# Lower projections of fifteen feed-forward pairs by Strassen's algorithm, with weight block sums made by accumulating transfers

## The chip, the cores and the metric

The kernel runs on one core of a Trainium2 chip. Time is the device time of one execution in microseconds (us); the time of a kernel is the median of its runs. The engines are TensorE (PE, matmuls; PEld is its weight load), VectorE (DVE), ScalarE (ACT), GpSimd (POOL) and SyncE (SP, which here only issues transfers).

## The reference

A trunk of two layers on 512 tokens and 1024 channels, all in float32. Layer 0 is a convolution module and a SwiGLU feed-forward part; then one set of keys and values is projected for the second layer; layer 1 is sliding-window attention and a second feed-forward part; a last normalisation ends it. Cut to what the change touches:

```python
def swiglu_ffn(x, w_up, w_down):
    gate, up = jnp.split(x @ w_up, 2, axis=-1)
    return (jax.nn.silu(gate) * up) @ w_down

for l in range(DEPTH):
    if l < N_A_LAYERS:
        h = h + conformer_conv(rmsnorm(h, norm_mix[l]), ...)
    else:
        if l == N_A_LAYERS:
            kv = rmsnorm(h, norm_kv) @ w_kv
        q = rmsnorm(h, norm_mix[l]) @ w_q[j]
        h = h + banded_sink_attention(q, k, v, sinks[j], rel_bias) @ w_o[j]
    h = h + swiglu_ffn(rmsnorm(h, norm_ffn[l]), w_up[l], w_down[l])
return rmsnorm(h, norm_final)
```

x is 512 x 1024, w_up 1024 x 5632 (gate and up), w_down 2816 x 1024.

## The kernel before

Everything is held transposed: channels on the 128 partitions, tokens along the free dimension. The running state h is eight tiles of 128 x 512. The hidden size of 2816 is eleven pairs of two 128-row tiles.

Each float32 factor is split into a high part in the faster float32r form and a low rest, and a product is three matmuls (`mm3`, L344 to L347): high by high, high by low, low by high. The activations are split once. The weights come as chunks of 128 x 1024 (512 KB): SP loads one into a `raw` tile, ACT casts it into `whi`, and DVE subtracts to get `wlo` (`split_chunk`, L261 to L271). There are four buffers each of `raw`, `whi` and `wlo`, so the cast of a chunk waits until PE has ended with the chunk four before it. `PLAN` is the list of all chunks in the order of use; `get` (L319) hands out the next one and first calls `advance`, which loads up to 6 chunks ahead and splits up to 3 ahead.

A feed-forward layer runs in parts of two to four pairs (`HALVES0`, `HALVES1`): all upper products of the part, then its lower projections, which add into h. The first two pairs of a layer are plain (`ffn_up`). All later pairs use Strassen's algorithm in Winograd's form for the upper products (`ffn_prod`, L573): seven products j = 0 to 6 on half-size blocks, which accumulate in three PSUM banks a, b and c, with moving factors of 256 tokens. The seven right factors (sums of blocks of the normalised state, `right_factors`) are formed once a layer. The left ones are weight blocks and their sums: `load_block` loads two blocks into `raw` and two into a `blocks` tile, and `block` (L219) forms S1, S3 and two more sums on DVE, two at j = 1 (L227, L228) and two at j = 2 (L231, L232).

The lower projections are plain (`down_group`, L468): for each half g of the output rows four banks of 128 x 512, for each pair two inner tiles, four row tiles, three matmuls of 512 tokens; then DVE adds each bank into h (L488). At the end of layer 0, `on_h` makes the normalised and split input of keys and values from each finished row tile (L458, L459) and POOL adds up its squares (L423).

The order of instructions on each engine is made by a scheduler ahead of time, and each engine runs its own list in order; PE's list mixes the next product in where the scheduler saw a use for it. So the order can be read, and does not change while the kernel runs.

Of the kernel before, what the change touches and what calls it, by code (L numbers as in the profile page):

```python
# [54 lines left out]
def chunk_plan():  # L55
# [42 lines left out]
    for kp in range(*LAST):  # L98
        for g in range(2):
# [4 lines left out]
PLAN = chunk_plan()  # L104
CHUNKS = [c for c in dict.fromkeys(PLAN) if c[0] != "prod"]
CHUNKS += [("up", layer, pair, half, which) for layer in range(2) for pair in range(PLAIN[layer], FT // 2)
           for which in range(2) for half in range(2)]
CHUNK_AT = {c: i for i, c in enumerate(CHUNKS)}


def lay_weights(w):
    out = np.empty((len(CHUNKS), P, 1024), np.float32)
    q = w["w_q"][0][:, HEAD_COLS]
    o = w["w_o"][0][HEAD_COLS, :]
    for i, c in enumerate(CHUNKS):
        if c[0] == "pw1":
            t = w["conv_w_pw1"][0].reshape(2, 4, P, 2, KT, P)[c[2], :, :, :, c[1]].reshape(4, P, 2 * P)
        elif c[0] in ("kv", "up", "q"):
            if c[0] == "q":
# [5 lines left out]
            t = src[half * 512:(half + 1) * 512, col:col + 256].reshape(4, P, 256)  # L125
# [6 lines left out]
        out[i].reshape(P, t.shape[0], t.shape[2])[...] = t.transpose(1, 0, 2)  # L132
    return out
# [39 lines left out]
def hybrid_trunk(ctx: ExitStack, tc: tile.TileContext, xT, W, prm_in, wdw_in, rnd_in, sinks, relb, onehot, fin, out):  # L173
# [28 lines left out]
    raws, splits = {}, {}  # L202
    str_pool = [None]
    DMA_AHEAD, SPLIT_AHEAD = 6, 3
    lo_engine = [nc.vector]
    split_limit, held = [2 * KT], [()]

    four = {}

    def load_block(i):  # L210
        _, layer, pair, j = PLAN[i]
        if j == 0:
            four[layer, pair] = str_pool[0].tile([P, 3, 1024], F32, tag="blocks", name=uid("blocks"))
        if j < 2:
            r = raws[i] = wpool.tile([P, 1024], F32, tag="raw", name=uid("raw"), bufs=4)
            nc.sync.dma_start(r, W[CHUNK_AT["up", layer, pair, j, 0]])
            nc.sync.dma_start(four[layer, pair][:, j], W[CHUNK_AT["up", layer, pair, j, 1]])

    def block(i):  # L219

        _, layer, pair, j = PLAN[i]
        b21, b22, s1 = (four[layer, pair][:, n] for n in range(3))
        a11, a12 = raws[i - j], raws.get(i - j + 1)
        if j == 0:
            return a11
        if j == 1:
            nc.vector.tensor_add(s1, b21, b22)  # L227
# [6 lines left out]
        if j == 6:  # L234
            raws.pop(i - 6), raws.pop(i - 5)
        return (s1, b21, a12, b22)[j - 3]

    def load(upto):
        while stream["dma"] < min(len(PLAN), upto):
            i = stream["dma"]  # L240
            if PLAN[i][0] == "prod":
                if str_pool[0] is None:
                    return
                load_block(i)
                stream["dma"] += 1
                continue
            r = wpool.tile([P, 1024], F32, tag="raw", name=uid("raw"), bufs=4)
            nc.sync.dma_start(r, W[CHUNK_AT[PLAN[i]]])
            raws[i] = r
            stream["dma"] += 1  # L250

    def advance():
        u = stream["use"]
        load(u + DMA_AHEAD)
        while stream["split"] < min(len(PLAN), u + SPLIT_AHEAD, split_limit[0]):
            i = stream["split"]
            if i >= stream["dma"]:
                return
            split_chunk(i)

    def split_chunk(i):  # L261
        r = block(i) if PLAN[i][0] == "prod" else raws.pop(i)
        stream["split"] = i + 1
        hi = wpool.tile([P, 1024], F32R, tag="whi", name=uid("whi"))
        lo = wpool.tile([P, 1024], F32R, tag="wlo", name=uid("wlo"))
        with ExitStack() as hold:
            for ins in held[0]:
                hold.enter_context(tc.issue_after(ins))
            done = (nc.scalar.copy(hi, r).ins, lo_engine[0].tensor_sub(lo, r, f32(hi)).ins)  # L269
        splits[i] = (hi, lo)  # L270
        return done  # L271
# [47 lines left out]
    def get(*key):  # L319
# [8 lines left out]
        hi, lo = splits.pop(i)  # L328
        n = {"pw1": 4, "kv": 4, "up": 4, "q": 4, "prod": 4}.get(key[0], 2)
        sh = dict(a=n)  # L330
# [149 lines left out]

    def ffn_part(layer, part, xg, rms=None, on_h=None):
        lo, hi = (HALVES0, HALVES1)[layer][part]
        hid = ffn_prod(layer, lo, hi, xg) if rms is None else ffn_up(layer, lo, hi, xg, rms)
        for g in range(2):
            banks = down_group([(("down", layer, kp, g), 2 * (kp - lo)) for kp in range(lo, hi)], lambda kt: hid[kt])
            for m in range(4):
                t = h[g * 4 + m]
                nc.vector.tensor_add(t, banks[m], t)  # L488
                if on_h is not None:
                    on_h(g * 4 + m)  # L490

    def ffn_up(layer, lo, hi, xg, rms):
# [28 lines left out]

    def right_factors(row, x):

        tiles = [str_pool[0].tile([P, 3, 1024], F32, tag="blocks", name=uid("blocks")) for _ in range(2)]
        b = [[t[:, n] for n in range(2)] for t in tiles]
# [46 lines left out]

    def ffn_prod(layer, lo, hi, xs):  # L573
        hid = Act(2 * (hi - lo))
        for pair in range(lo, hi):
            a, b, c = (bank() for _ in range(3))
            g1, g2 = temp(), temp()

            def halves(t):
                return t.rearrange("p (m s) -> p m s", m=2)  # L580

            def hidden(u, g, tok):
                i = 2 * (pair - lo)
                nc.vector.scalar_tensor_tensor(g, u, -1.0, g, op0=ALU.mult, op1=ALU.mult)
                split(tuple(q[:, i % 4:i % 4 + 2, tok] for q in hid.q[i // 4]), halves(g))
# [29 lines left out]
            product(6, a, False, True)  # L615
            hidden(a, g1, HALF[0])
        return hid

    class Next:
# [12 lines left out]
        def later(self):  # L632
            for g in self.gains[1:]:
                self.x[g] = Act(KT)
                for i in range(KT):
                    split_scaled(self.x[g][i], h[i], col(g, i))
                    yield
# [352 lines left out]
    attn = ExitStack()  # L990
    table_pool = attn.enter_context(tc.tile_pool(name="table", bufs=1))
    bias = table_pool.tile([P, NH, BAND], F32, tag="bias", name="bias", bufs=1)
    blocks = ExitStack()
    str_pool[0] = blocks.enter_context(tc.tile_pool(name="blocks", bufs=2))

# [6 lines left out]

    base = seen[0]
    job(read_bias(), (base + 6, 0), (base + 36, 9))

    def factors(gain, n, x):
        for _ in range(4):
            yield
# [5 lines left out]

        yield from right_factors(row, x)

    def ffn_parts(layer, parts, n, on_h=None):
        gain = n.gains[0]
        right = {}
        background.append(factors(gain, n, right))  # L1020
        rate[0] = 1.5
        ffn_part(layer, 0, n.x[gain], n.rms)
        flush()
# [8 lines left out]
    if True:  # L1032
        ffn_parts(0, 4, n0, nxt.on_h)
        blocks.close()
        str_pool[0] = None
        at = attn.enter_context(tc.tile_pool(name="attn", bufs=2))
# [8 lines left out]
        for half in range(2):  # L1045
            whi, wlo = get("kv", 0, half)
            for k in range(4):
                for m in range(2):
                    sl = slice(m * P, (m + 1) * P)
                    mm3(kb[m], (whi[:, k, sl], wlo[:, k, sl]), xkv[half * 4 + k],  # L1050
                        half == 0 and k == 0, half == 1 and k == 3)
        rms.step1()
        vb = [bank() for _ in range(4)]
        for half in range(2):
            whi, wlo = get("kv", 1, half)
            for k in range(4):
                xh, xl = xkv[half * 4 + k]
                for n in range(4):
# [152 lines left out]
    attn.close()  # L1211
    blocks = ExitStack()
    str_pool[0] = blocks.enter_context(tc.tile_pool(name="blocks", bufs=2))

    right = ffn_parts(1, 3, nxt)
    hid = ffn_prod(1, *LAST, right)
    blocks.close()

# [94 lines left out]
```

## Time and profile before

| | |
|---|---|
| median of 3 runs | 1056.72 us (1055.94 to 1058.72) |
| the profiled execution | 1053.6 us |
| its span | 1051.8 us |
| matmuls of 128x256 on L345, L346, L347 | about 0.28 us each, pipelined |
| matmuls of 128x512 on the same lines | about 0.39 us each, pipelined |

A line of the profile's fifth part reads: line of the kernel, engine, operation, output from inputs, shape, count; then busy time in all and the mean of one; then the idle time of that engine just ahead of it, and whose end ended it. Matmuls overlap in the array, so the distance between two starts says more of PE than the duration of one. In a row of windows each engine has its busy time and, in brackets, the number of its instructions. The chain lists the work that ended last, followed back from the end.

### The profile page before, as it was taken

To read this page: it belongs to the slowest core of one execution; us is meant where nothing else is said; L and a number is where in the kernel's file an instruction comes from. 1 tells how busy PE (TensorE), PEld (TensorE's weight loads), DVE (VectorE), ACT (ScalarE), POOL (GpSimd) and SP (SyncE) were. 2 spreads that over 40 slices of the span, in tenths; PEclk is the share of its full clock that TensorE was granted. 3 is DMA by queue.
4 is the path that set the end of the run, shared out by engine and by line. 5 is a ranking of instruction groups with operands and counts; after the bars stand their busy time and mean duration, and the time that the engine had idled before them with its cause. 6 is when DMAs were issued, how large, how long until landed. Compare 5 with 4: busy or idle time off the path is not lost.

```text
span 1051.8 us, 16099 instructions
## 1 busy us (share of the span) xinstructions
PE 1037.6 (99%) x6492; PEld 899.4 (86%) x6492; DVE 754.4 (72%) x981; ACT 501.4 (48%) x765; POOL 184.5 (18%) x200
## 2 busy tenths in 40 slices
PE   9999999999999999999999999999999999999997
PEld 7666568888998999899879878788899988998996
DVE  8799857599776587576684677578977754776663
ACT  6666645352552355155453766345355432542443
POOL 0799801311000000000130534041100000000000
PEclk9999999999999999999999999999999999999999
DMA  7656675324244124221323120232323431342112
GB/s 256 179 160 180 148 139 120 100 80 141 81 124 138 63 98 160 61 81 62 120 81 100 61 61 22 80 105 87 131 98 105 140 118 41 109 145 88 41 61 80
DMA packets 36918, 111.64 MB, mean 106 GB/s; under 512 B 4395, under 2 KB 7260, under 8 KB 36828
## 3 DMA queue, kind: packets, MB, share of 16 engines
q1 hardware_dynamic: 35692, 109.32, 35.0%
q10 hardware_dynamic: 1152, 1.29, 0.4%
q8 instruction: 51, 0.84, 0.3%
q14 instruction: 23, 0.19, 0.1%
HBM read 106.25 MB, written 4.73 MB: 106 GB/s over the span
## 4 chain that ended last, share of the span: by engine, by line
PE 88%; DVE 2%; issue 1%; ACT 1%; POOL 0%; POOLq 0%; ACTq 0%
PE bank L346 23%; PE bank L345 23%; PE bank L347 23%; PE bank L337 18%; PE bank L1242 2%; DVE quad L459 1%; DVE wlo L269 1%; ACT whi L269 0%; PE bank L450 0%; PE bank L1232 0%; PE bank L433 0%; DVE h L488 0%; DVE quad L280 0%; POOL rr L908 0%; ACT tmp L280 0%
## 5 line engine op out<-in xcount | busy, mean ns | idle before, releaser
L346 PE MATMUL bank<-quad,whi 128*128 128x256 f32 (+1 forms) x1536 | 488.5, 320 | 1.3 <-DVE quad L459 0.9
L345 PE MATMUL bank<-quad,whi 128*128 128x256 f32 (+1 forms) x1536 | 483.9, 320 | 0.3 <-ACT tmp L606 0.3
L347 PE MATMUL bank<-quad,wlo 128*128 128x256 f32 (+1 forms) x1536 | 482.6, 320 | 0.0
L269 ACT CAST whi<-raw 128x1024 fp32r<-128x1024 f32 x174 | 182.5, 1050 | 294.8 <-PE bank L346 197.4
L346 PEld LDWEIGHTS bank<-quad,whi 128*128 128x128 f32 x1536 | 292.6, 190 | 22.8 <-DVE quad L459 1.3
L345 PEld LDWEIGHTS bank<-quad,whi 128*128 128x128 f32 x1536 | 291.3, 190 | 23.0 <-ACT quad L280 0.7
L347 PEld LDWEIGHTS bank<-quad,wlo 128*128 128x128 f32 x1536 | 290.0, 190 | 20.2
L269 DVE TENSOR_TENSOR wlo<-raw,whi 128x1024 fp32r<-128x1024 f32 x174 | 220.5, 1270 | 112.4 <-ACT whi L269 110.1
L337 PE MATMUL bank<-quad,whi 128*128 128x512 f32 x512 | 160.9, 395 | 0.6 <-ACT whi L280 0.6
L337 PEld LDWEIGHTS bank<-quad,whi 128*128 128x128 f32 x512 | 94.8, 188 | 26.7 <-issue 4.0
L269 DVE TENSOR_TENSOR wlo<-blocks,whi 128x1024 fp32r<-128x1024 f32 x54 | 65.5, 1221 | 57.5 <-ACT whi L269 57.5
L269 ACT CAST whi<-blocks 128x1024 fp32r<-128x1024 f32 x54 | 56.6, 1048 | 91.7 <-PE bank L346 69.4
L337 PE MATMUL bank<-quad,wlo 128*128 128x512 f32 x256 | 99.9, 390 | 0.1
L824 POOL TENSOR_TENSOR quad<-quad 128x512 f32<-128x512 f32 x53 | 76.4, 1442 | 10.9 <-ACT quad L822 7.8
L337 PEld LDWEIGHTS bank<-quad,wlo 128*128 128x128 f32 x256 | 48.1, 188 | 10.7 <-DVE wlo L280 0.4
L1253 POOL TENSOR_TENSOR rs<-ss,mhalf 128x1 f32<-128x1 f32 x4 | 2.2, 549 | 298.0 <-DVE ss L1251 298.0
L423 POOL TENSOR_TENSOR tmp<-tmp,tmp 128x512 f32<-128x512 f32 x21 | 32.9, 1568 | 111.8 <-ACT tmp L421 100.5
L1115 POOL COPY sc<-sk 128x4 f32<-128x4 f32 x16 | 3.6, 256 | 257.1 <-DVE wlo L269 254.9
L822 ACT ACTIVATE quad<-apad,wdw 128x512 f32<-128x512 f32 x53 | 36.7, 718 | 17.8 <-POOL quad L824 17.8
L1139 POOL TENSOR_SCALAR sc<-sc,sm 128x256 f32<-128x256 f32 (+1 forms) x64 | 31.8, 518 | 65.9 <-DVE sm L1137 62.6
L488 DVE TENSOR_TENSOR h<-bank,h 128x512 f32<-128x512 f32 x56 | 37.1, 683 | 8.6 <-PE bank L347 8.5
L1135 ACT ACTIVATE sc<-sc,m 128x257 f32<-128x257 f32 (+1 forms) x64 | 30.2, 475 | 22.5 <-DVE m L1126 22.5
(168 smaller groups left out, 1010.5 us busy)
## 6 DMA issues: line engine op xcount, KB each, us to landing
raw<-in_W_dram SPq DMA_DIRECT2D x139, 512.0 KB, 3.6
blocks<-in_W_dram SPq DMA_DIRECT2D x36, 512.0 KB, 4.4
shifted<-rowsd SPq DMA_DIRECT2D x16, 262.0 KB, 5.4
shifted<-rowsd SPq DMA_DIRECT2D x12, 260.0 KB, 5.2
rowsd<-apad SPq DMA_DIRECT2D x8, 271.0 KB, 3.3
bias<-fd SPq DMA_DIRECT2D x8, 256.0 KB, 10.3
h<-in_xT_dram SPq DMA_DIRECT2D x3, 512.0 KB, 6.7
shifted<-rowsd SPq DMA_DIRECT2D x4, 264.0 KB, 4.8
```

Of the source, the lines that this page charges most:

```text
L269: done = (nc.scalar.copy(hi, r).ins, lo_engine[0].tensor_sub(lo, r, f32(hi)).ins)
L337: turn[0] = nc.tensor.matmul(*args, **kw).ins
L345: nc.tensor.matmul(out, w[0], x[0], start=start, stop=False, **kw)
L346: nc.tensor.matmul(out, w[0], x[1], start=False, stop=False, **kw)
L347: nc.tensor.matmul(out, w[1], x[0], start=False, stop=stop, **kw)
L423: eng.tensor_add(sq, self.acc[eng], sq)
L488: nc.vector.tensor_add(t, banks[m], t)
L822: nc.scalar.mul(pr, src, self.tap(j))
L824: nc.gpsimd.tensor_add(to, acc, pr)
L1135: nc.scalar.activation(sc[:, j, 0:1 + w], sc[:, j, 0:1 + w], AF.Exp, bias=self.m4[:, j:j + 1], scale=-1.0, accum_out=sm[:, j:j + 1])
L1139: nc.gpsimd.tensor_scalar(sc[:, j, 1:1 + w], sc[:, j, 1:1 + w], sm[:, j:j + 1], 0.0, op0=ALU.mult, op1=ALU.add)
L1242: nc.tensor.matmul(self.banks[g], x, w[:, k, :], start=False, stop=kp == LAST[1] - 1 and k == 1 and n == 2)
```

## The change

The lower projections of fifteen pairs, five groups of three (layer 0's pairs 2 to 10, layer 1's 3 to 8), also use Strassen's algorithm (`down_prod`). Each half of the row tiles (ms = 0, 1) is one block problem: the output is four row tiles (two upper, two lower) by two halves of the tokens, the inner size three pairs. Seven products of 18 matmuls with 256 tokens go into three banks a, b and c; after each product DVE adds a bank into h or takes it away (`add`), and a and c go on accumulating, so that some parts of h are added twice. The weight chunks for it are 128 x 768.

- The hidden pairs are kept as seven right factors each (`Rights`): `finish` forms them on DVE and splits them, in place of the plain split in `hidden`.
- At the turn from upper products to lower (ms = 0), products 0, 1 and 3 first run over the first two pairs and only then over the last pair.
- The sums S1 and S3 of the weight blocks come from accumulating transfers that POOL issues (`accum_op=ALU.add`), for upper and lower blocks; DVE keeps the two sums at j = 2.
- In these stages up to nine chunks are loaded ahead, and `load` holds a chunk back until its buffer's last reader has been put down.
- `HALVES1` takes three pairs in its first part, of which the third is a Strassen pair with plain lower projections.
- The keys' and values' chunks take the row tiles in the order in which they end (`KV_ORDER`), and `on_h` is called for two tiles at a time.
- The attention bias table is read at the key and value stage, not during the second pointwise product and layer 0's first part.

```diff
-HALVES1 = ((0, 2), (2, 6), (6, 9))
+HALVES1 = ((0, 3), (3, 6), (6, 9))
+N_DOWN = 3
+D_ORDER = (0, 1, 3, 2, 4, 5, 6)
+KV_ORDER = (0, 1, 4, 5, 2, 3, 6, 7)
...
         ups(layer, lo, hi)
+        if lo:
+            plan.extend(("dprod", layer, (lo, ms), j) for ms in range(2) for j in D_ORDER)
+            return
...
+            f = four[kind, layer, key]
+            r = four[kind, layer, key, j] = wpool.tile([P, 1024], F32, tag="raw", name=uid("raw"), bufs=4)
+            nc.sync.dma_start(r[:, 0:w], part(j, 0))
+            nc.sync.dma_start(f[:, j, 0:w], part(0, 1))
+            nc.gpsimd.dma_start(f[:, j, 0:w], part(1 - j, 1 - j), accum_op=ALU.add)
+            if j:
+                nc.sync.dma_start(f[:, 2, 0:w], part(1, 1))
...
         if j == 1:
-            nc.vector.tensor_add(s1, b21, b22)
-            nc.vector.tensor_add(b21, a11, b21)
             return a12
...
+        def finish(self, b1, b2):
+
+            self.add()
+            t = halves(temp())
+            nc.vector.tensor_sub(t[:, 0], b1[:, 0], b2[:, 0])
+            nc.vector.tensor_sub(t[:, 1], b2[:, 1], b2[:, 0])
+            self.put(0, b1)
+            nc.vector.scalar_tensor_tensor(b2[:, 0], t[:, 0], -1.0, b2[:, 1], op0=ALU.mult, op1=ALU.subtract)
+            self.put(2, b2)
+            self.put(4, t)
+            nc.vector.scalar_tensor_tensor(b1[:, 1], b2[:, 0], -1.0, b1[:, 1], op0=ALU.mult, op1=ALU.subtract)
+            self.put(6, b1[:, 1:2])
...
+    def down_prod(layer, lo, hid, on_h):
+        last = N_DOWN - 1
+        for ms in range(2):
+            a, b, c = (bank() for _ in range(3))
...
+            split_ahead[0] = 2
+            parts = [(j, get("dprod", layer, (lo, ms), j), dst) for j, dst in zip(D_ORDER[:3], (a, b, c))]
+            split_ahead[0] = 3
+            for ks in (range(last), [last]) if ms == 0 else (range(N_DOWN),):
+                for (j, w, dst), half, tok, op in zip(parts, (0, 0, 1), (HALF[0], HALF[0], HALF[1]),
+                                                      (ALU.add, ALU.add, ALU.subtract)):
+                    product(j, w, dst, ks, ks[0] == 0, j == 1 and ks[-1] == last)
+                    if ks[-1] == last:
+                        add(half, tok, dst, op)
+            whole(2, a, False, False)
+            add(0, HALF[1], a)
+            whole(4, a, False, False)
+            add(1, HALF[1], a, ALU.subtract)
+            whole(5, c, False, True)
+            add(0, HALF[1], c)
...
+            whole(6, a, False, True)
+            add(1, HALF[0], a, ALU.subtract)
...
-    base = seen[0]
-    job(read_bias(), (base + 6, 0), (base + 36, 9))
...
+        job(read_bias(), (seen[0], 0), (seen[0] + 4, 9))
```

What that makes of the engines' lists is shown at three places, all in layer 0; the names end in the buffer's number, and `[waits ...]` names the engine or queue whose semaphore a row waits for. The first is PE at the turn between the two halves of output rows, in the second group. Before (whi479 is the last chunk of the first half, whi483 the first of the second; whi483 takes the buffer of whi466, which PE last read 66 rows earlier):

```order
L345 MATMUL bank477_3685<-quad401_2998,whi479_3688 128x512
L346 MATMUL bank477_3685<-quad402_2999,whi479_3688 128x512
L347 MATMUL bank477_3685<-quad401_2998,wlo480_3689 128x512
L345 MATMUL bank488_3783<-quad399_2996,whi483_3720 128x512 [waits PE_49]
L346 MATMUL bank488_3783<-quad400_2997,whi483_3720 128x512
L347 MATMUL bank488_3783<-quad399_2996,wlo484_3721 128x512
```

After (product 2 of the first half ends in bank498, product 5 begins in bank500, and bank518 is product 0 of the second half; whi512 takes the buffer of whi504):

```order
L383 MATMUL bank498_3898<-hid496_3884,whi504_3912 128x256
L384 MATMUL bank498_3898<-hid495_3883,wlo505_3913 128x256
L382 MATMUL bank500_3900<-quad443_3405,whi508_3977 128x256 [waits DVE_49,Activation_49]
L383 MATMUL bank500_3900<-quad444_3406,whi508_3977 128x256
L382 MATMUL bank518_4074<-quad443_3405,whi512_4023 128x256 [waits Activation_49]
L383 MATMUL bank518_4074<-quad444_3406,whi512_4023 128x256
L384 MATMUL bank500_3900<-quad443_3405,wlo509_3978 128x256 [waits DVE_49]
```

Two matmuls of the next half's first product have moved in two rows behind the last use of the buffer that their weights take. The second place is DVE in the same group. Before, the four adds into h that end the first half, and the splits around them:

```order
L269 TENSOR_TENSOR wlo493_3788<-raw478_3686,whi492_3787 128x1024 [waits DMAHW1_49,PE_49,Activation_49]
L488 TENSOR_TENSOR h_75<-bank474_3682,h_75 128x512 [waits PE_49]
L488 TENSOR_TENSOR h_75<-bank475_3683,h_75 128x512 [waits PE_49]
L488 TENSOR_TENSOR h_75<-bank476_3684,h_75 128x512 [waits PE_49]
L488 TENSOR_TENSOR h_75<-bank477_3685,h_75 128x512 [waits PE_49]
L269 TENSOR_TENSOR wlo495_3816<-raw482_3717,whi494_3815 128x1024 [waits Activation_49]
```

After, in the second half (bank518 is a, bank519 b and bank520 c; bank498 is product 6 of the first half; wlo525, 527 and 529 belong to products 2, 4 and 5):

```order
L306 TENSOR_TENSOR wlo525_4089<-raw492_3850,whi524_4088 128x768 [waits Activation_49]
L586 TENSOR_TENSOR h_75<-h_75,bank498_3898 128x2x256 [waits PE_49]
L586 TENSOR_TENSOR h_75<-h_75,bank519_4075 128x2x256 [waits DVE_49,PE_49]
L306 TENSOR_TENSOR wlo527_4150<-blocks491_3849,whi526_4149 128x768 [waits DMASW3_49,Activation_49]
L306 TENSOR_TENSOR wlo529_4154<-raw501_3901,whi528_4153 128x768 [waits Activation_49]
L586 TENSOR_TENSOR h_75<-h_75,bank520_4076 128x2x256 [waits PE_49]
```

The add of bank520, which product 5 needs ahead of it, stands behind three splits and two adds; before, nothing that PE accumulated into later had to be added first. The third place is POOL's list from the end of the convolution stage on (names without numbers). Before, the four products with the activated gate in layer 0's first part are next to each other:

```order
L437 TENSOR_TENSOR rs_1714<-ms_1712,mhalf 128x4
L502 TENSOR_TENSOR tmp_1789<-tmp_1788,tmp_1789 128x512
L502 TENSOR_TENSOR tmp_1797<-tmp_1796,tmp_1797 128x512
L502 TENSOR_TENSOR tmp_1948<-tmp_1947,tmp_1948 128x512
L502 TENSOR_TENSOR tmp_1956<-tmp_1955,tmp_1956 128x512
```

After, the accumulating transfers stand among them, and follow one another through the rest of the layer:

```order
L474 TENSOR_TENSOR rs_1714<-ms_1712,mhalf 128x4
L240 DMA blocks_1906<-in_W_dram 128x1024 x2
L632 TENSOR_TENSOR tmp_1787<-tmp_1786,tmp_1787 128x512
L632 TENSOR_TENSOR tmp_1795<-tmp_1794,tmp_1795 128x512
L632 TENSOR_TENSOR tmp_1946<-tmp_1945,tmp_1946 128x512
L240 DMA blocks_2112<-in_W_dram 128x1024 x2
L632 TENSOR_TENSOR tmp_1954<-tmp_1953,tmp_1954 128x512
L240 DMA blocks_2302<-in_W_dram 128x1024 x2
```

Two issues have moved in front of the first of these products, and two in front of the last.

More of the change, by code (lines that the diff above doesn't have):

```diff
@@ L104 @@
 PLAN = chunk_plan()
-CHUNKS = [c for c in dict.fromkeys(PLAN) if c[0] != "prod"]
+CHUNKS = [c for c in dict.fromkeys(PLAN) if "prod" not in c[0]]
 CHUNKS += [("up", layer, pair, half, which) for layer in range(2) for pair in range(PLAIN[layer], FT // 2)
+           for which in range(2) for half in range(2)]
+CHUNKS += [("dn", layer, key, half, which) for _, layer, key, j in (c for c in PLAN if c[0] == "dprod") if j == 0
            for which in range(2) for half in range(2)]
@@ L118, in lay_weights @@
         elif c[0] in ("kv", "up", "q"):
+            order = KV_ORDER if c[0] == "kv" else range(KT)
             if c[0] == "q":
@@ L479, in down_group, with ffn_part @@
         return banks
[L481 removed]
+    def ffn_part(layer, part, xg, rms=None, on_h=None, right=None):
         lo, hi = (HALVES0, HALVES1)[layer][part]
[L483 removed]
+        if lo:
+            down_prod(layer, lo, ffn_prod(layer, lo, hi, xg, Rights()), on_h)
+            return
+        plain = PLAIN[layer]
+        hids = [ffn_up(layer, lo, plain, xg, rms)]
+        if hi > plain:
+            flush()
+            hids.append(ffn_prod(layer, plain, hi, right))
+        hid = [t for pairs, n in zip(hids, (plain - lo, hi - plain)) for t in (pairs[i] for i in range(2 * n))]
         for g in range(2):
@@ L520, in ffn_up, with right_factors @@
         return hid
-    def right_factors(row, x):
-        tiles = [str_pool[0].tile([P, 3, 1024], F32, tag="blocks", name=uid("blocks")) for _ in range(2)]
+    def right_factors(row, x, tiles):
         b = [[t[:, n] for n in range(2)] for t in tiles]
@@ L1001, in read_bias, with factors @@
                                       ap=[[NH * 3 * P - 1, 16], [3 * P, NH], [1, BAND]]))
-    base = seen[0]
-    job(read_bias(), (base + 6, 0), (base + 36, 9))
-    def factors(gain, n, x):
-        for _ in range(4):
+    def factors(gain, n, x, idle, tiles):
+        for _ in range(idle):
             yield
@@ L1019, in ffn_parts @@
         right = {}
-        background.append(factors(gain, n, right))
-        rate[0] = 1.5
-        ffn_part(layer, 0, n.x[gain], n.rms)
+        factors_on[0] = True
+        tiles = [str_pool[0].tile([P, 3, 1024], F32, tag="blocks", name=uid("blocks")),
+                 hid_pool[0].tile([P, 2, 1024], F32, tag="hid", name=uid("hid"))]
+        block_until.append(-1)
+        idle, rate[0] = ((4, 1.5), (6, 2))[layer]
+        background.append(factors(gain, n, right, idle, tiles))
+        ffn_part(layer, 0, n.x[gain], n.rms, right=right)
         flush()
```

149 lines of the change are left out of this document (106 added, 43 removed).

## The prediction

> **What bounds the kernel now.** I read the page's first part and its chain, then the windows around one group, then PE's waits and the chain at the end of layer 0.
>
> ```profile
> PE 1037.6 (99%) x6492; PEld 899.4 (86%) x6492; DVE 754.4 (72%) x981; ACT 501.4 (48%) x765; POOL 184.5 (18%) x200
> PEclk9999999999999999999999999999999999999999
> PE 88%; DVE 2%; issue 1%; ACT 1%; POOL 0%; POOLq 0%; ACTq 0%
> 259.00:322.90 63.90, 63.90 (x519) 63.20 (x518) 47.52 (x51) 32.83 (x41) 0.00 (x0) 1.00 0.36 116
> 322.90:352.90 30.00, 30.00 (x134) 24.81 (x134) 18.11 (x20) 6.61 (x8) 0.00 (x0) 1.00 0.29 88
> PE bank L346 <- DVE quad L459: 0.9, 1, 0.9
> PE bank L345 <- ACT tmp L606: 0.3, 1, 0.3
> ```
>
> PE is the bound: busy 99% of the span, at full granted clock, and 88% of the chain. The two windows are one group of three pairs in layer 0, the upper products (259 to 322.9) and the lower projections (322.9 to 352.9; columns: PE, PEld, DVE, ACT, POOL, clock, DMA share, GB/s). PE never pauses in either, while DVE works 47.5 + 18.1 = 65.6 of 93.9 us, 70%. The last two rows are all that PE waited for between 480 and 560 us, across the end of layer 0: 1.2 us. So fewer PE columns are worth their full price only if the engines that feed PE still keep up at every turn.
>
> **What PE is spared.** Three start times from the timeline give the steps; columns are start, then a pipelined duration that I don't use.
>
> ```profile
> 309.26 0.28 PE L347 MATMUL bank<-quad,wlo 128*128 128x256 f32 x1
> 309.38 0.28 PE L345 MATMUL bank<-quad,whi 128*128 128x256 f32 x1
> ...
> 310.58 0.28 PE L347 MATMUL bank<-quad,wlo 128*128 128x256 f32 x1
> ...
> 352.20 0.39 PE L345 MATMUL bank<-quad,whi 128*128 128x512 f32 x1
> 352.42 0.39 PE L346 MATMUL bank<-quad,whi 128*128 128x512 f32 x1
> 352.65 0.39 PE L347 MATMUL bank<-quad,wlo 128*128 128x512 f32 x1
> 352.88 0.28 PE L345 MATMUL bank<-quad,whi 128*128 128x256 f32 x1
> ```
>
> Eleven steps of the 256-column form take 1.32 us, 0.120 each; three of the 512-column form take 0.68, 0.227 each. A group's plain lower projections are 3 pairs x 2 column halves x 8 x 3 = 144 matmuls of 512: 32.7 us. By Strassen they are 2 x 7 products x 18 = 252 of 256: 30.2 to 30.4 us. That is 2.35 us a group, and five groups are changed: **-11.8 us**. Everything else on PE keeps its count.
>
> The Trainium skill weighs differently here: "TensorE: Matmul & The Clock Gate", section "Wait — 56ns, not 53.3ns?", gives a warm step of the columns over 2.4 GHz plus about 2.5 ns, so 109 and 216 ns, and by it the saving would be 31.1 - 27.5 = 3.6 us a group, 17.8 in all, and the sum below 6 us lower. The trace doesn't agree: both steps are some 11 ns longer, which weighs twice where matmuls are halved, so the measured steps stand.
>
> **What DVE and ACT get.** Rows of DVE and ACT between 259 and 540 us, and one short form:
>
> ```profile
> L269 DVE TENSOR_TENSOR wlo<-raw,whi 128x1024 fp32r<-128x1024 f32 x54 | 66.2, 1226 | 33.2 <-ACT whi L269 33.1
> L488 DVE TENSOR_TENSOR h<-bank,h 128x512 f32<-128x512 f32 x26 | 17.5, 685 | 4.4 <-PE bank L347 4.3
> L227 DVE TENSOR_TENSOR blocks<-blocks 128x1024 f32<-128x1024 f32 x7 | 8.6, 1223 | 3.8 <-DMA blocks<-in_W_dram 3.8
> L269 ACT CAST whi<-raw 128x1024 fp32r<-128x1024 f32 x54 | 56.8, 1052 | 101.8 <-PE bank L346 73.3 <-issue 27.7
> L462 ACT CAST quad<-tmp 128x512 fp32r<-128x512 f32 x18 | 10.4, 619 | 0.0
> L280 DVE TENSOR_TENSOR wlo<-raw,whi 128x256 fp32r<-128x256 f32 x4 | 1.7, 419 | 0.1
> ```
>
> The new weight tiles are 768 wide. DVE's price lies between 0.685 (512) and 1.226 (1024), ACT's between 0.62 and 1.05; I take the middles, 0.955 and 0.83. Per group DVE loses 6 weight block adds and 6 wide splits (2 x 7.3 us), 8 adds into h (5.5) and 6 factor splits (4.1), and gains 14 splits (13.4), 4 block adds (3.8), 14 adds into h (9.6) and the right factors: per pair four short operations at 0.42, three splits at 0.685 and one at 0.42, 12.5 in all. So 65.6 becomes about 80.7 of some 91.5 us, 88%. As an average that hides under PE; at the turns it need not.
>
> **The turn from upper to lower.** After product 6 of the last pair DVE has fourteen operations before the lo part that PE needs 74 matmuls, 8.8 us, later: an evacuation and three adds into h of 512, three splits of 512, three of 768, four short ones. Their busy times sum to 9.35; back to back DVE starts the next 0.07 to 0.08 earlier, so 8.3. I cost the turn at nothing, hidden by the 36 matmuls on the first two pairs (4.3 us) and the three rests: a margin of 0.5 us. A margin gone is the slower rival.
>
> **The turn between the two halves of rows (ms).** In the order after, two matmuls on whi512 stand two rows behind the last use of whi504, and whi tiles rotate through four buffers (504, 506, 508, 510, 512), so that cast can begin only then. What such a release costs is in the chain at the end of layer 0:
>
> ```profile
> 534.46 0.24 PE bank L346
> 534.77 1.06 ACT whi L269
> 535.85 1.22 DVE wlo L269
> 537.08 0.61 DVE h L488
> ```
>
> The cast starts 0.31 after the matmul's start and ends 1.06 later. With 0.83 for the narrower one whi512 is there 1.15 to 1.25 us after the last matmul's start, and PE wants it after three steps, 0.36: a wait of 0.8 to 0.9 that nothing covers, since PE runs in order. Five groups have the same rows: 5 x 0.9 = **+4.5**. Before, the like turn had 66 matmuls of cover.
>
> **The third bank in the second half.** Product 5 goes on into bank520, so DVE must first have added it to h. That add stands behind the splits of wlo525, 527 and 529 and two adds; wlo525 follows the cast into whi524, released by the last matmul of the first half's product 6. From that matmul: 0.35 + 0.83 for the cast, 3 x 0.87 and 2 x 0.61 for the queue ahead (back to back), 0.69 and a release for the add: 5.8 us. PE arrives after 39 matmuls, 4.7 us. Wait: 1.1. If the 768 forms cost as little as 512 ones it is 0.2, at the 1024 price 2.0. Four groups have this order: 4 x 1.1 = **+4.4**. The add of product 2's bank follows, but PE comes to it only 20 matmuls later, covered.
>
> **End of layer 0.** The fifth group runs into keys and values, where each finished row tile costs DVE an L459 beside POOL's adds, and all of the new h adds stand among them.
>
> ```profile
> L459 DVE SCALAR_TENSOR_TENSOR quad<-h,prm,quad 128x512 fp32r<-128x512 f32 x6 | 6.9, 1166 | 0.2
> 498.00:552.00 54.00, 52.74 (x267) 44.73 (x266) 38.47 (x42) 28.25 (x41) 12.57 (x11) 1.00 0.32 98
> ```
>
> Before, PE is idle for 1.3 us there (54.00 - 52.74). After, product 2 of the second half uses a whi tile two matmuls behind its release (0.85), product 5's add is short of about 0.55, and the first lo part of the key weights stands behind four h adds, three splits and five L459: 1 to 3 us by where POOL slows them; I take 1.9. So 3.3 for about 1.9, the 1.3 and 0.6 of short pauses: **+1.4**, between -1 and +4.
>
> **Transfers.**
>
> ```profile
> q1 hardware_dynamic: 35692, 109.32, 35.0%
> raw<-in_W_dram SPq DMA_DIRECT2D x139, 512.0 KB, 3.6
> blocks<-in_W_dram SPq DMA_DIRECT2D x36, 512.0 KB, 4.4
> bias<-fd SPq DMA_DIRECT2D x8, 256.0 KB, 10.3
> ```
>
> Of the weight blocks four transfers become seven for each of 18 upper pairs (28 MB more), and ten lower blocks bring 27.5 MB in place of 15.7. About 149 MB at the same rate is 48% of the time: volume is no bound. No accumulating transfer, and none from POOL, stands in this trace. I take the plain 4.4 us, above it the 10.3 of the slowest kind, below it nothing; the sums are first wanted by product 2, 7 to 9 us after a plain landing, so both ends are hidden. On POOL, idle in these windows (0.00), the issues delay only L502's four products in each layer's first part, by a microsecond or two beside upper products. The bias loads move to the key stage, some 50 us ahead of their use: nothing.
>
> **Sum.** -11.8 + 4.5 + 4.4 + 1.4 = -1.5. The profiled execution took 1053.6 (span 1051.8), 3.1 under the median of 1056.72; on it the sum gives 1052.1, on the median **1055.2**.
>
> **Rivals.**
> - *The second wait is absorbed* (768 forms nearer 512): only the ms turns and layer end cost: -11.8 + 4.5 + 1.4 = -5.9, 1050.8. For it: DVE idles 12 us in each window of 30 before. Against: the queue's order is fixed.
> - *No wait shows* (releases earlier than the chain's 0.31, or PE's look-ahead): -11.8 to -10, 1045 to 1047. Against: PE starts nothing past an unready matmul in the rows above.
> - *DVE is late at every group's turn* (slower). If its fourteen operations take their busy times and three of them wait for a fresh cast, 9.35 + 3 x 0.3 = 10.3, against 8.8: 1.5 us late, five times, +7.5: 1062.7. It decides where the fourteen exceed 8.8 us. For it: 88% load. Against: back-to-back starts in the trace.
> - *Accumulating transfers land late* (slower): beyond about 9 us after the plain load PE waits for product 2, at 28 blocks; each microsecond over costs 28, so 1080 or more. Against: DMA is 35% busy and POOL free. The Trainium skill, "SBUF — State Buffer", section "Who interferes with whom", says that GpSimd's descriptors starve while DVE holds a two-port mode, and that tensor_tensor has none; no run here shows either, and were it otherwise this rival would grow.
> - That the change doesn't do what it says is excluded by the order: the products are there.
>
> **How the numbers follow.** The forecast, 1052 to 1059 by the bounds of its prices, has 0.47; the second wait absorbed 0.22; none 0.13; DVE late 0.12; transfers late 0.06. A measurement of this kernel can tell about 0.3%, 3.2 us, from no change. Faster than 1053.5: the two better rivals and 0.07 of the forecast, 0.42. Slower than 1059.9: both slower ones and 0.03, 0.21. The rest, 0.37, is no change. The range leaves out the late transfers and the outer halves of two others: 1046 to 1062.5; the forecast's own is 1052 to 1059.
>
> **What would show it.** PE's matmuls of 256 should step at 0.120 in the lower products as above. At the ms turn PE should wait 0.9 for ACT's whi, five times; ahead of product 5 about 1.1 for DVE's h, four times. If PE's idle time in a group is under 1 us, the second step is wrong; if over 3, DVE is later than I have it, or a transfer is, which the releasers tell. A landing over 12 us for the accumulating loads would make the whole wrong.

## The result, and the profile after

The changed kernel takes 1066.54 us (four runs, 1065.2 to 1067.09) beside 1056.33 for the kernel before: a ratio of 1.0091, 95% interval 1.0076 to 1.0106. It is slower, outside the predicted range. Its profiled execution spans 1063.4 us. First the busy times and the transfers of the page of the changed kernel (q0 is the queue of POOL's transfers; the last column of an issue row is the time to landing):

```profile
PE 1034.4 (97%) x7032; PEld 919.2 (86%) x7032; DVE 812.3 (76%) x1125; ACT 542.4 (51%) x835; POOL 233.3 (22%) x256
q0 software_dynamic: 8064, 26.74, 14.8%
blocks<-in_W_dram POOLq DMA_DIRECT2D x36, 512.0 KB, 7.9
blocks<-in_W_dram POOLq DMA_DIRECT2D x20, 384.0 KB, 5.4
```

PE fell from 99% to 97% busy: it waits now. Next, what PE waited for in the whole span (us in total, times, longest):

```profile
PE bank L382 <- ACT quad L495: 8.0, 1, 8.0
PE bank L384 <- DVE wlo L306: 3.1, 2, 1.7
PE bank L382 <- ACT whi L306: 2.8, 5, 0.6
...
PE bank L382 <- ACT tmp L734: 1.1, 3, 0.4
```

One wait of 8.0 us stands out. Before, PE's longest wait at the keys and values was 0.9 (the row with L459 in the prediction). The timeline at that place, PE, DVE, ACT and SP of the changed kernel (start, duration; in brackets the idle time ahead and what ended it):

```profile
532.78 4.07 SPq L1139 DMA_DIRECT2D bias<-fd  x8
539.25 78.41 SPq L284 DMA_DIRECT2D raw<-in_W_dram  x13
...
548.59 0.39 PE L384 MATMUL bank<-quad,wlo 128*128 128x512 f32 x1
548.96 0.68 DVE L586 TENSOR_TENSOR h<-h,bank 128x512 f32<-128x512 f32 x1
555.25 1.05 ACT L306 CAST whi<-raw 128x1024 fp32r<-128x1024 f32 x1 [10.28 <-DMA raw<-in_W_dram]
556.21 0.72 ACT L495 ACTIVATE quad<-h,prm 128x512 fp32r<-128x512 f32 x1
...
556.98 1.22 PE L382 MATMUL bank<-quad,whi 128*128 128x512 f32 x2 [8.00 <-ACT quad L495]
...
558.87 0.63 PE L384 MATMUL bank<-quad,wlo 128*128 128x512 f32 x1
559.29 0.63 PE L383 MATMUL bank<-quad,whi 128*128 128x512 f32 x1
559.72 0.63 PE L384 MATMUL bank<-quad,wlo 128*128 128x512 f32 x1
```

Read it from the end. PE waits for ACT's L495, the split of the last row tiles for keys and values. Their last add into h (L586) is done at 549.6. But ACT runs in order, and ahead of L495 stands a cast that has been waiting 10.28 us for its weights: the first load that SP issued behind the eight transfers of the bias table (539.3). It landed at 555.2. The windows of the same stretch (PE, PEld, DVE, ACT, POOL, clock, DMA share, GB/s):

```profile
540.00:545.00 5.00, 5.00 (x28) 4.29 (x27) 5.00 (x4) 3.61 (x5) 2.82 (x2) 1.00 1.15 119
545.00:550.00 5.00, 3.98 (x23) 3.16 (x21) 4.63 (x7) 0.00 (x0) 2.88 (x4) 1.00 1.15 116
550.00:555.00 5.00, 0.00 (x0) 0.00 (x0) 0.00 (x0) 0.00 (x0) 0.00 (x0) 0.82 1.07 217
555.00:560.00 5.00, 2.95 (x6) 1.94 (x7) 3.67 (x4) 4.55 (x7) 2.33 (x2) 0.50 0.84 309
```

The DMA engines are full (share over 1) while they move only 116 to 119 GB/s: the table's transfers, in runs of 1 KB, are slow. For five microseconds no engine works at all. Then the granted clock is 0.50 and the 512-column matmuls above start 0.43 us apart, not 0.227. So the stop costs some 3 us more after it ends: nine matmuls with 0.2 too much each, and three starts that take 1.2 too much together.

### The profile page after: what moved, and what is told of

Its sections match the earlier page's. It is cut to its first block, busy times and chain, and to the rows that moved or that the text cites. A ratio compares the mean times of both kernels' runs of the same rounds, so it can differ in the third digit from the quotient of the medians.

```text
span 1063.4 us, 17692 instructions
## 1 busy us (share of the span) xinstructions
PE 1034.4 (97%) x7032; PEld 919.2 (86%) x7032; DVE 812.3 (76%) x1125; ACT 542.4 (51%) x835; POOL 233.3 (22%) x256
## 4 chain that ended last, share of the span: by engine, by line
PE 85%; DVE 3%; issue 2%; DMA 1%; ACT 1%; POOL 0%; POOLq 0%; ACTq 0%; DVEq 0%
PE bank L382 22%; PE bank L383 21%; PE bank L384 21%; PE bank L374 18%; PE bank L1383 2%; DMA raw<-in_W_dram 1%; DVE wlo L306 1%; ACT whi L306 1%; DVE quad L496 1%; DVE h L586 0%; PE bank L487 0%; PE bank L470 0%; PE bank L1373 0%; DVE raw L256 0%; ACT tmp L734 0%
## 5 line engine op out<-in xcount | busy, mean ns | idle before, releaser
L382 PE MATMUL bank<-quad,whi 128*128 128x256 f32 (+1 forms) x1576 | 471.9, 305 | 12.1 <-ACT quad L495 8.0
L383 PE MATMUL bank<-quad,whi 128*128 128x256 f32 (+1 forms) x1576 | 475.4, 303 | 0.1
L384 PE MATMUL bank<-quad,wlo 128*128 128x256 f32 (+1 forms) x1576 | 471.6, 303 | 3.1 <-DVE wlo L306 3.1
L382 PEld LDWEIGHTS bank<-quad,whi 128*128 128x128 f32 x1576 | 300.0, 191 | 27.5 <-ACT quad L495 8.4
L383 PEld LDWEIGHTS bank<-quad,whi 128*128 128x128 f32 x1576 | 301.2, 191 | 12.5 <-DVE quad L496 0.8
L306 ACT CAST whi<-raw 128x1024 fp32r<-128x1024 f32 (+1 forms) x184 | 184.7, 1005 | 233.2 <-PE bank L383 139.5
L306 DVE TENSOR_TENSOR wlo<-raw,whi 128x1024 fp32r<-128x1024 f32 (+1 forms) x184 | 222.0, 1209 | 81.6 <-ACT whi L306 77.5
L240 POOL DMA_DIRECT2D blocks<-in_W_dram x56 | 49.3, 898 | 498.7 <-DMA blocks<-in_W_dram 133.7
L306 ACT CAST whi<-blocks 128x1024 fp32r<-128x1024 f32 (+1 forms) x84 | 81.8, 974 | 116.4 <-PE bank L383 109.6
L306 DVE TENSOR_TENSOR wlo<-blocks,whi 128x1024 fp32r<-128x1024 f32 (+1 forms) x84 | 97.7, 1164 | 40.1 <-ACT whi L306 39.8
L374 PEld LDWEIGHTS bank<-quad,whi 128*128 128x128 f32 x512 | 95.0, 189 | 26.1 <-issue 3.8
L586 DVE TENSOR_TENSOR h<-h,bank 128x512 f32<-128x512 f32 x70 | 47.1, 684 | 16.7 <-PE bank L384 16.5
L500 DVE TENSOR_TENSOR quad<-tmp,quad 128x512 fp32r<-128x512 f32 (+1 forms) x62 | 41.0, 674 | 4.0 <-ACT quad L499 4.0
```

Source lines behind the costliest of these rows:

```text
L240: nc.gpsimd.dma_start(f[:, j, 0:w], part(1 - j, 1 - j), accum_op=ALU.add)
L374: turn[0] = nc.tensor.matmul(*args, **kw).ins
L382: nc.tensor.matmul(out, w[0], x[0], start=start, stop=False, **kw)
L383: nc.tensor.matmul(out, w[0], x[1], start=False, stop=False, **kw)
L384: nc.tensor.matmul(out, w[1], x[0], start=False, stop=stop, **kw)
L500: nc.vector.tensor_sub(dst[1], src, f32(dst[0]))
```

## Where the transfers and the wait meet

Four kernels test theory A (the bias transfers cause the wait) against B (the new order at the keys and values does); a fifth tests the path from the one to the other.

**bias_late.** The eight transfers are queued behind the weight loads that come next:

```diff
+            last_load[0] = nc.sync.dma_start(r, W[CHUNK_AT[PLAN[i]]]).ins
...
-        job(read_bias(), (seen[0], 0), (seen[0] + 4, 9))
+        job(read_bias(), (seen[0] + 1, 0), (seen[0] + 4, 9))
...
+            with tc.issue_after(last_load[0]):
                 nc.sync.dma_start(bias[p:p + 16, :, :], ...)
```

> The change, with the eight bias transfers queued on SP behind the weight loads that come next (two, three and three of them between the loads for the query weights) and not ahead of them. Theory A: the 8.0 us that PE waits at the keys and values, and the low clock behind it (about 4 us), come from the bias transfers sharing the queues with the last key and value weights. Then that wait is under 1 us, the clock stays at 1.00 and the time is 1054 to 1056.5. Rival B: the wait is of the new order itself (keys and values take tiles as finished, factors held up behind ACT and DVE): the wait stays at 7 to 9 us and the time at 1065 to 1067.

Measured: 1057.54 us, ratio to before 1.0007 (0.9995 to 1.002). What PE waited for in bias_late:

```profile
PE bank L384 <- DVE wlo L306: 4.0, 2, 2.5
PE bank L382 <- ACT whi L306: 2.8, 5, 0.6
...
PE bank L382 <- ACT quad L495: 1.5, 1, 1.5
```

The 8.0 us are 1.5 and the clock stays at 1.00, and 9.0 us of the time are gone. The wait is a little longer than A expected; the time, 1 us above the top of A's range, has its rest elsewhere (below).

**bias_none.** No table at all:

```diff
-        job(read_bias(), (seen[0], 0), (seen[0] + 4, 9))
+        nc.gpsimd.memset(bias, 0.0)
```

> The change without reading the bias table: POOL clears the tile in place of the eight transfers, so scores have no bias and no mask. A: as without any wait, 1053 to 1056, no PE wait over 2 us around the keys and values. B: 1065 to 1067. The difference to bias_late says what the transfers still cost where they are put later.

Measured: 1057.51, ratio 1.0009 (0.9995 to 1.0023), as bias_late: put there, the transfers cost nothing more. A's own range ended 1.5 lower, and the wait for L495 is 2.2 us.

**bias_plain.** The same 2 MB in long runs at the old place:

```diff
-                nc.sync.dma_start(bias[p:p + 16, :, :], bass.AP(...))
+                nc.sync.dma_start(bias[:, 4 * g:4 * g + 4, :].rearrange("p a b -> p (a b)"), W[g])
```

> The change, with four plain transfers of 512 KB of weights into the bias tile at the same place (the same 2 MB in long runs, so the scores get other numbers). If the short runs of 1 KB are what makes the table slow (8 x 256 KB took some 20 us at about 110 GB/s), 2 MB at the weights' rate takes 7 us, PE waits 0 to 2 us and the time is 1054 to 1057. If it is the mere volume or the place in the queue, PE waits 5 us or more and the time is above 1060. B: 1065 to 1067.

Measured: 1057.04, ratio 1.0006 (0.9995 to 1.0016); the wait for L495 is 1.5 us again. So it is the form of the table's transfers and not their 2 MB: they landed after 13.4 us (median), these after 7.5. That the short runs alone make the difference is not shown: the table's eight transfers also fill 16 partitions each, and each partition's rows start one element off the last one's.

**before_bias_kv.** The kernel before with its table read there too, behind the key and value chunks:

```diff
-    base = seen[0]
-    job(read_bias(), (base + 6, 0), (base + 36, 9))
...
+        job(read_bias(), (seen[0], 0), (seen[0] + 4, 9))
...
+            with tc.issue_after(load_ins["kv", 1, 1]):
                 nc.sync.dma_start(bias[p:p + 16, :, :], ...)
```

> The kernel before, with nothing changed but that its eight bias transfers are read at the keys and values, on SP behind their four weight chunks, as in the change. A: they hold up the weights there too: 1060 to 1068, with a PE wait of 4 us or more near 550 us. B: 1055 to 1058, as before.

Measured: 1055.79, ratio 0.9993 (0.9982 to 1.0005). A missed, and B's range held: the move alone costs nothing in the old kernel. The timelines of SP and ACT in before_bias_kv say why:

```profile
496.98 26.14 SPq L248 DMA_DIRECT2D raw<-in_W_dram  x7
523.18 5.35 SPq L1000 DMA_DIRECT2D bias<-fd  x8
530.68 68.80 SPq L248 DMA_DIRECT2D raw<-in_W_dram  x12
...
549.53 0.71 ACT L458 ACTIVATE quad<-h,prm 128x512 fp32r<-128x512 f32 x1
550.14 1.04 ACT L269 CAST whi<-raw 128x1024 fp32r<-128x1024 f32 x1
```

There the table starts at 523 and the next load, the first query chunk, lands at 547.7, 7.5 us earlier beside an end of layer 0 that comes at the same time. In the change the `raw` tiles come free later, by the splits of the lower products: the last of the key and value weights is issued 8.5 us later (531.3 for 522.8) and the table 9.6. And there the cast of that chunk (550.14) stands behind the last split for keys and values (549.53) in ACT's list, not ahead of it, so a later landing would not have held up that split. Which of the two would have been enough alone was not tested.

**after_cast_held.** The change with its transfers where it has them; only the cast of the first query chunk is queued on ACT behind the splits of the last row tiles:

```diff
-            for ins in held[0]:
+            for ins in (tile_in if PLAN[i] == ("q", 0, 0) else held[0]):
                 hold.enter_context(tc.issue_after(ins))
...
-            split_scaled(self.x[g][i], h[i], col(g, i))
+            tile_in[0] = split_scaled(self.x[g][i], h[i], col(g, i))
```

> The change with its bias transfers where it has them, and one thing moved: ACT's cast of the first query chunk, whose load stands behind the bias transfers and lands at 555 us, is queued behind the splits of the last two row tiles and not ahead of them. Theory: the late load reached PE only through that place in ACT's list. Then the wait of 8.0 us becomes that of bias_late (1.5 to 2.5), with the transfers as late as before, and the time is 1056.5 to 1058.5. Rival: the key weights themselves are late, or the query chunk is late for its own use: 1062 to 1067.

Measured: 1057.52, ratio 1.0007 (0.9995 to 1.0019). ACT's timeline of after_cast_held:

```profile
548.56 0.72 ACT L495 ACTIVATE quad<-h,prm 128x512 fp32r<-128x512 f32 x1 [4.68 <-DVE h L587]
...
553.95 1.05 ACT L306 CAST whi<-raw 128x1024 fp32r<-128x1024 f32 x1 [3.00 <-DMA raw<-in_W_dram]
```

The load is as late as before (ACT still waits for it, until 553.95), but the splits for keys and values stand ahead of it, and 9.0 us are gone. The key and value weights themselves, which A named, were not late: in the changed kernel ACT cast the last of them at 543.92. That settles the cause: a late transfer, an instruction that waits for it, and the work of another kind queued behind that instruction.

## Where the saving on PE went

Without that stop the change is level with the kernel before, so some 12 us, all of its PE saving, are spent elsewhere. Six kernels look for them; five start from bias_late.

**late_held.** The first product of the second half is queued behind product 5 of the first:

```diff
+                    with tc.issue_after(gate) if ms and j == 0 else nullcontext():
                         mm3(dst[:, m * 256:(m + 1) * 256], ...)
...
             whole(5, c, False, True)
+            gate = last_mm[0]
```

> bias_late, with the first product of the second half of rows queued on PE behind product 5 of the first half, so that its two early matmuls stand 18 further on, well after the buffer of their weights is free. If the five pauses of 0.7 us at these turns are that cast and nothing else, they go (PE waits for whi at 128x256 fall from 2.8 us to under 0.5) and the time falls by 3 to 4 us to 1053 to 1054.5. If DVE's wlo for product 5 ends no earlier (rival: the cast only covers a wait that is there anyway), PE waits for DVE's wlo as long and the time stays at 1057.

Measured: 1055.87, ratio 1.0000 (0.9987 to 1.0012). The five waits for whi are gone from late_held's list, but

```profile
PE bank L384 <- DVE wlo L306: 4.9, 7, 2.1
```

shows seven waits for wlo where bias_late had two: five of them, gaps of 0.58 for 0.12, are the same turns. Half theory, half rival: behind the cast DVE's split of product 5 is late as well, by some 0.46 us. The time is not told apart from bias_late's (1.0007).

**late_gate_dve.** Layer 1's four products of gate and up value on DVE:

```diff
-                nc.gpsimd.tensor_mul(t2, t1, t2)
+                (nc.vector if len(stages) else nc.gpsimd).tensor_mul(t2, t1, t2)
```

> bias_late, with layer 1's four products of gate and up value on DVE and not on POOL (four of about 0.7 us more for DVE). Theory: the 6.3 us that two wlo splits take there (2.4 elsewhere) come from POOL reading beside DVE, so without POOL's products they take 2.4 to 3.5, PE's wait of 2.65 us at 752 and the lower clock after it fall to under 1, and the time falls by 1.5 to 4 us to 1053.5 to 1056. Rival: the POOL-issued transfers alone cause it, or DVE is simply full there: the wait stays above 2 and the time at 1057 or above.

Measured: 1054.57, ratio 0.9984 (0.9973 to 0.9995). bias_late's timeline at the place, DVE and POOL:

```profile
746.53 0.68 DVE L631 TENSOR_TENSOR tmp<-bank,rsbc 128x512 f32<-128x512 f32 x1
749.47 5.17 DVE L306 TENSOR_TENSOR wlo<-blocks,whi 128x1024 fp32r<-128x1024 f32 x1
...
749.14 0.93 POOL L240 DMA_DIRECT2D blocks<-in_W_dram  x1 [21.31 <-DVE quad L661]
749.80 1.60 POOL L632 TENSOR_TENSOR tmp<-tmp,tmp 128x512 f32<-128x512 f32 x1
751.04 1.20 POOL L240 DMA_DIRECT2D blocks<-in_W_dram  x1
751.64 1.90 POOL L632 TENSOR_TENSOR tmp<-tmp,tmp 128x512 f32<-128x512 f32 x1
```

late_gate_dve's, and then the kernel before's:

```profile
751.23 1.21 DVE L306 TENSOR_TENSOR wlo<-blocks,whi 128x1024 fp32r<-128x1024 f32 x1
...
751.38 1.87 POOL L240 DMA_DIRECT2D blocks<-in_W_dram  x2 [39.38 <-DVE wlo L306]
...
741.22 2.02 DVE L269 TENSOR_TENSOR wlo<-raw,whi 128x1024 fp32r<-128x1024 f32 x1
...
740.87 1.30 POOL L502 TENSOR_TENSOR tmp<-tmp,tmp 128x512 f32<-128x512 f32 x1 [16.14 <-DVE tmp L501]
```

Of the two splits that the expectation put at 6.3 us together, one is slow: beside two of POOL's products and its issues it takes 5.17 us; beside issues alone 1.21, as elsewhere; beside one product alone 2.02 in the kernel before, where PE does not wait. The seven traces that have both at this place show 4.3 to 5.2. So the products slow the split, and the issues bring two of them together: the issue at 749.14 waits for DVE's L661, and the first product, whose factor from L631 was ready at 747.2, starts only behind it. PE's wait there is gone, and with it the low clock that followed. The Trainium skill, "SBUF — State Buffer", section "Who interferes with whom", has that a DVE tensor_tensor with both inputs in SBUF contends with GpSimd's reads, and infers that descriptor writing needs another interface; the rows with products alone and with issues alone agree.

**late_sums_dve.** S1 and S3 by DVE adds again:

```diff
-            nc.sync.dma_start(f[:, j, 0:w], part(0, 1))
-            nc.gpsimd.dma_start(f[:, j, 0:w], part(1 - j, 1 - j), accum_op=ALU.add)
-            if j:
-                nc.sync.dma_start(f[:, 2, 0:w], part(1, 1))
+            nc.sync.dma_start(f[:, 2 * j, 0:w], part(j, 1))
...
+            nc.vector.tensor_add(s3, a11, s1)
+            nc.vector.tensor_add(s1, s1, a22)
```

> bias_late, with the sums S1 and S3 of the weight blocks made by two DVE adds again, for upper and lower blocks, and no accumulating transfer: four transfers a block, not seven. If the accumulating transfers buy DVE the time that the lower products need (theory), DVE is late at turns of every group: +5 to +15, 1062 to 1072. If they are as good as neutral, 1056 to 1059. If their issue on POOL is what delays the start of layer 1 (2.65 us of waiting at 752), that pause goes whatever the rest does.

Measured: 1055.88, ratio 0.9993 (0.9981 to 1.0006), not told apart from bias_late. A miss: PE waits at a turn of each of four groups (its list has `PE bank L381 <- ACT whi L305: 4.1, 4, 1.0`, at 1.18 a gap), for casts that themselves wait until PE lets go of their buffer. But the three waits for ACT's L734 are gone, and so is the wait at the start of layer 1, as the last clause had it: with no issue between them POOL's two products start 3.1 us apart, and the slowest split there takes 2.31 us. late_gate_dve took out the products, this kernel the issues; either is enough.

**before_accum.** That part alone, on the kernel before:

```diff
-            nc.sync.dma_start(four[layer, pair][:, j], W[CHUNK_AT["up", layer, pair, j, 1]])
+            nc.sync.dma_start(f[:, j], W[CHUNK_AT["up", layer, pair, 0, 1]])
+            nc.gpsimd.dma_start(f[:, j], W[CHUNK_AT["up", layer, pair, 1 - j, 1 - j]], accum_op=ALU.add)
...
-            nc.vector.tensor_add(s1, b21, b22)
-            nc.vector.tensor_add(b21, a11, b21)
```

> The kernel before with one part of the change alone: S1 and S3 of the upper blocks by accumulating transfers from POOL, two DVE adds a block less, seven transfers for four. PE had no waits there, so theory: nothing to gain, 1055 to 1058; DVE's share falls by some 4% of the span. Rival, that the accumulating transfers are late for product 2 or disturb the weight loads: 1060 or more.

Measured: 1059.06, ratio 1.0021 (1.0008 to 1.0034): DVE fell from 72% to 68%, and the time rose by some 2 us. No single pause of PE explains it: 34 pauses of under 0.3 us (start to start, over the normal step) sum to 4.2 us in the two feed-forward parts, beside 22 and 1.5 before. The eleven longest, five of 0.27 and six of 0.15, each wait for ACT's copy of a bank (L608), which stands behind the wide cast of a block sum, like the waits for L734 in the change.

**late_kv_old.** The keys' order undone:

```diff
-KV_ORDER = (0, 1, 4, 5, 2, 3, 6, 7)
+KV_ORDER = tuple(range(8))
```

> bias_late, with keys and values taking the tiles in their numbered order (the change's last clause undone). The second half of layer 0's last group then has to give tiles 2 and 3 before key products go on. Theory: worth 1 to 4 us at that turn, so 1058 to 1061.5. Rival, that the order is neutral: 1056.5 to 1058.

Measured: 1061.8, ratio 1.0052 (1.0034 to 1.0071), 4.3 to 4.8 above bias_late (by the times, and by the ratios). In its list the wait for ACT's L495 has become

```profile
PE bank L383 <- DVE quad L496: 3.0, 1, 3.0
```

and slow matmuls follow it. So taking the tiles as they end is worth its place, a little over what was expected.

**late_both.** late_held and late_gate_dve together.

> bias_late with the two moves that each helped, late_held and late_gate_dve. If they act at different places they add: 0.9 to 1.7 us each below bias_late, so 0.25 to 0.4% faster than the kernel before, 1052.5 to 1054. If the pauses only move on, it is no faster than late_gate_dve.

Measured: 1053.23, ratio 0.9965 (0.9953 to 0.9977). It is faster than both kernels. Together the two moves bring 0.42% of bias_late, alone 0.07 and 0.23, so nothing is lost between them; late_held's part alone is within its noise.

## Why the prediction was wrong

The step that failed is one sentence: "The bias loads move to the key stage, some 50 us ahead of their use: nothing." I priced when the table is needed, not what it pushes back. It cost 9.0 us (1066.54 to 1057.5, by moving the transfers, by dropping them, by long runs or by moving one cast). The row with the 10.3 us landing of a 256 KB table piece stood in the prediction; the load behind eight of them and the ACT list behind that load were not followed.

Point by point, against bias_late, which has the rest of the change:

- PE's saving: the steps are 0.120 and 0.227 as before, so the -11.8 holds. The Trainium skill's steps of 109 and 216 ns, "TensorE: Matmul & The Clock Gate", section "Wait — 56ns, not 53.3ns?", fit neither kernel.
- Turn from upper to lower, nothing: right, but three times an upper product of the next group waits about 0.5 for ACT's copy behind a wide cast (L734): 1.5 us that I didn't have.
- The ms turns, +4.5: right in place and cause, five waits; a gap of 0.83 for 0.12 is 0.71 each, 3.6 in all. late_held shows that DVE would have cost most of it anyway.
- The third bank, +4.4: nothing. I let whi524 wait for whi510's buffer, by strict rotation. ACT and DVE in bias_late show otherwise:

```profile
339.88 0.84 ACT L306 CAST whi<-raw 128x768 fp32r<-128x768 f32 x1 [1.11 <-PE bank L383]
...
341.17 0.95 DVE L306 TENSOR_TENSOR wlo<-raw,whi 128x768 fp32r<-128x768 f32 x1
343.99 1.28 DVE L586 TENSOR_TENSOR h<-h,bank 128x512 f32<-128x512 f32 x2 [1.86 <-PE bank L384]
```

The cast starts at 339.88, 4 us ahead of the end of product 6 of the first half (the add at 343.99 waits for it). So it had a buffer that came free earlier, and the queue ahead of the add was a cast and a split shorter.

- End of layer 0, +1.4: two gaps of 1.85 and 1.86 and a short stretch of slow starts in bias_late, about 3.7 beyond the normal steps, less the 1.9 of before: +1.8.
- Start of layer 1: I had POOL's issues "delay only L502's four products". They did delay one, so that two ran beside one split on DVE, and that was the cost: 2.65 us of waiting and 1.4 of low clock.
- Accumulating transfers: landing after 7.9 and 5.4 us (medians), above the 4.4 that I took and within the bound of 10.3; three of 56 exceeded it, the longest with 12.5 (I had taken any over 12 as a sign of being wrong; two are), and no wait of PE is put down directly to one of these landings. They are not free on their own (before_accum).

So the terms give -11.8 + 3.6 + 1.5 + 1.8 + 4.0 = -0.9 for bias_late, which measured +0.6; the 1.5 between is in no term. The forecast of -1.5 was near that by luck, by errors that cancel: 5.3 too much (third bank, ms turns) and 5.9 too little. The rivals had DVE late at every group's turn, which did not come, and no rival for a transfer ahead of a weight load.

## What to carry to other kernels

When a transfer moves, follow the load behind it to the instruction that waits for it, and then read what stands behind that instruction in its engine's list: an in-order engine turns one late load into a wait for all that follows. Of a transfer, price how long it fills the queues, by its landing time in the trace, and not only its bytes. Buffers of a pool are not to be counted by rotation without a look at the casts: here one began 4 us before rotation would have let it.

## What the runs showed of the hardware

A pause decides the clock well before 8 us. In the convolution stage, which the change leaves alone, the profiled executions of before and of the changed kernel differ at one place. Before:

```profile
84.89 2.35 PE L337 MATMUL bank<-shifted,tables 128*32 128x512 f32 x20 [1.85 <-DVE wlo L269]
```

After:

```profile
85.06 2.36 PE L374 MATMUL bank<-shifted,tables 128*32 128x512 f32 x12 [2.17 <-DVE wlo L306]
```

With a wait of 1.85 us 20 matmuls start in the next 2.35 us, with 2.17 only 12. All thirteen traces have this place. In the four with a wait of 1.63 to 2.03 us the 32 matmuls behind it take 3.64 us. In eight of the nine with 2.17 to 2.59 they take 5.34, at a granted clock of 0.50; the ninth, 2.29 in before_bias_kv, leaves the clock up. So the line lies just above 2 us here and is not sharp. Likewise the two waits of 1.5 us at the keys in bias_late leave the clock up, while at the start of layer 1, where PE stands 2.65 us beyond its step, the 256-column steps after it are 0.21. The Trainium skill, "TensorE: Matmul & The Clock Gate", section "What's actually happening", gives an idle window of about 3.4 us; these waits are shorter, and the measurement decides. It makes a pause just above 2 us cost 1.5 to 1.8 times itself (2.17 and 1.70 behind it; 2.65 and 1.4).
